# A feed-forward on one core with seven block products in place of eight

## Chip, core and metric

One Trainium2 chip, one core. The metric is the time of one execution on the device, in microseconds. Times come from three runs of the kernel and from one execution with the hardware profiler on.

## What is computed

One layer of a diffusion backbone over 1024 latent tokens (width 1024) with 256 context tokens. A token-mixing sub-layer (a gated linear recurrence and a windowed attention, merged by gates, projected by `w_out`) is added to the stream; then the feed-forward, which is what the change touches:

```python
x_new = x + g1 * _merge(y_hg, y_at, gates, w_branch_hgrn, w_branch_attn, w_out)
h = _modulate(x_new, norm_ffn_w, sh2, sc2)          # (1024, 1024)
out = x_new + g2 * ((silu(h @ w_gate) * (h @ w_up)) @ w_down)
# w_gate, w_up: (1024, 2816); w_down: (2816, 1024); all fp32
```

## The kernel before

Every large product is made from split operands: a value is rounded to `fp32r` (its high part, `act.copy`), the rest is the low part (`dve.tensor_tensor` subtraction), and high x high, high x low and low x high are accumulated in one PSUM bank, three matmuls for one. The matmuls are put in the written order by `InOrder` (L76, L79); on the other engines, and on the queues that issue transfers, a scheduler fixes the order of instructions ahead of the run, from what it takes to be ready first.

Up to about 840 us the kernel does the modulation, the input projections, the attention and the recurrence. Then `gen_ba` (L1048) multiplies the attention branch, L1143 to L1165 multiply the recurrence branch (`bh`) and merge both with gates that are loaded in pairs of pages (`ga`, `gb`), and `project(nh, bs)` (L1238) applies `w_out` to one block of 128 tokens, for one half of 512 columns: 24 matmuls of 512 columns. `project(0, ...)` runs for all blocks, then `project(1, ...)`; after a block's second half, `second_norm` (L1195) squares it (ScalarE), finds the scale (POOL) and scales it (VectorE). `norm_late` (L1256) runs a product and puts the block's eight transposes and its modulation and split (`second_norm_t`, L1209) behind 18 of the 24 matmuls, so block b is transposed inside the product of block b+1; block 6 and block 7 are transposed inside the first two products of the feed-forward.

The feed-forward goes through `w_gate`, `w_up` and `w_down` in 22 blocks of 128 hidden columns. `up(f)` (L1278) loads and splits 512 KB of `w_gate` and of `w_up`, and for each half t of the tokens runs 24 matmuls for the gate and 24 for up (`gemm_ch`, k outer, three terms inner), takes Silu of the gate, multiplies, and splits the result into `ah`, `al`. It also loads a row block of `w_down`, multiplies it by g2 on POOL and splits it. `down(parts, blocks, last)` (L1303) multiplies two such hidden blocks: for each token block and column half 2 x 3 matmuls into one bank; then it adds the bank to the residual page `xn[b]` (L1315), which stays in SBUF. Downs run one pair behind; the last one stores the output (L1317). Weight pages have three buffers (`whi`, `wlo`) and two for what is loaded (`wraw`).

## Time and profile before

| | |
|---|---|
| median of 3 runs | 1756.8 us (1756.18 to 1760.09) |
| the profiled execution | 1757.2 us |
| its span, first to last instruction | 1755.4 us |
| mean granted TensorE clock | 0.985 of full speed |
| instructions | 22971, of which 8820 matmuls |
| DMA | 192.6 MB, mean 110 GB/s |

The rows further down come from the profiled execution. Times are us from the start of the span unless marked ns. PE is TensorE, PEld its weight loads, DVE VectorE, ACT ScalarE, POOL GpSimd, SPq the issuing of transfers on SyncE. L1315 is line 1315 of the kernel before; `out<-in` are the program's tile names, xN a count. Where matmuls are pipelined, the mean of one is its latency, not its spacing.

### The profile page before, as it was taken

The page shows a single profiled execution, that of the slowest core. Times are in us where ns is not written, and L with a number is a line of the kernel's source. Part 1 is how long each engine was busy: PE and PEld are TensorE (multiplying, and loading weights), DVE is VectorE, ACT ScalarE, POOL GpSimd, SP SyncE. Part 2 cuts the span into 40 slices and gives each one's busy share as a digit, 9 for nine tenths or more (in the row PEclk, how much of TensorE's full clock was granted, in tenths as well). Part 3 has the DMA queues.
Part 4 walks back from the last instruction along what each step waited for, and adds up shares of the span by engine and source line. Part 5 has one row for each costly group of instructions (what it writes and reads, how often), then busy time and mean ns, then how long its engine had stood idle before and what let it go on. Part 6 is the DMA issues. An engine that isn't in the chain of part 4 may idle for free. (4 is left out here: it accounts for less than half of the span.)

```text
span 1755.4 us, 22971 instructions
## 1 busy us (share of the span) xinstructions
PE 1692.5 (96%) x8820; PEld 1411.9 (80%) x8820; DVE 958.4 (55%) x1831; ACT 622.7 (35%) x1178; POOL 329.7 (19%) x361
## 2 busy tenths in 40 slices
PE   6899999999889999999899999999999999999999
PEld 4689889998778787788677788888888888888887
DVE  3863577777769697964277462333333433423324
ACT  4312355556546465644543352111112112112110
POOL 2402635310012222321334111010010010010000
PEclk8899999999999999999999999999999999999999
DMA  9771312123277465623555102111112112112102
GB/s 366 252 278 39 110 45 86 46 85 118 93 239 239 133 232 172 228 96 103 191 182 184 36 26 73 47 49 57 40 48 60 36 49 60 37 48 60 37 12 96
DMA packets 177205, 192.60 MB, mean 110 GB/s; under 512 B 9311, under 2 KB 131264, under 8 KB 177096
## 3 DMA queue, kind: packets, MB, share of 16 engines
q1 hardware_dynamic: 161544, 168.59, 29.8%
q10 hardware_dynamic: 15552, 22.55, 3.5%
q8 instruction: 69, 1.13, 0.3%
q14 instruction: 40, 0.33, 0.1%
HBM read 146.53 MB, written 44.57 MB: 109 GB/s over the span
## 5 line engine op out<-in xcount | busy, mean ns | idle before, releaser
L76 PE MATMUL pu<-h,whi_fu 128*128 128x512 f32 x704 | 216.8, 389 | 0.0
L76 PE MATMUL pg<-h,whi_fg 128*128 128x512 f32 x704 | 216.8, 389 | 0.0
L1296 POOL TENSOR_TENSOR fd<-fd,g 128x1024 f32<-128x1024 f32 x22 | 52.7, 2394 | 589.6 <-DMA fd<-in_w_ffn_down_dram 589.6
L1315 DVE TENSOR_TENSOR xn<-xn,dn 128x512 f32<-128x512 f32 x176 | 119.5, 685 | 76.0 <-PE dn L76 75.8
L76 PEld LDWEIGHTS pg<-h,whi_fg 128*128 128x128 f32 x704 | 132.1, 188 | 27.5
L76 PEld LDWEIGHTS pu<-h,whi_fu 128*128 128x128 f32 x704 | 132.1, 188 | 27.2
L76 PE MATMUL pg<-h,wlo_fg 128*128 128x512 f32 x352 | 136.9, 389 | 0.0
L76 PE MATMUL pu<-h,wlo_fu 128*128 128x512 f32 x352 | 136.9, 389 | 0.0
L76 PE MATMUL dn<-dh,ah 128*128 128x512 f32 x352 | 136.9, 389 | 0.0
L76 PE MATMUL dn<-dl,ah 128*128 128x512 f32 x352 | 136.9, 389 | 0.0
L76 PE MATMUL dn<-dh,al 128*128 128x512 f32 x352 | 136.9, 389 | 0.0
L1289 DVE TENSOR_TENSOR sv<-sv,pu 128x512 f32<-128x512 f32 x44 | 30.3, 688 | 192.7 <-PE pu L76 191.2
L76 PE MATMUL g<-hhi,whi_g 128*128 128x512 f32 x256 | 110.0, 430 | 2.8 <-ACT gs_g L347 2.7
L76 PE MATMUL g<-hhi,wlo_g 128*128 128x512 f32 x256 | 101.4, 396 | 0.0
L76 PE MATMUL g<-hlo,whi_g 128*128 128x512 f32 x256 | 100.9, 394 | 0.0
L1288 ACT ACTIVATE sv<-pg 128x512 f32<-128x512 f32 x44 | 26.0, 592 | 208.5 <-PE pg L76 208.5
L76 PE MATMUL wo<-wop,mh 128*128 128x512 f32 x256 | 79.5, 392 | 0.0
L76 PEld LDWEIGHTS pu<-h,wlo_fu 128*128 128x128 f32 x352 | 66.0, 188 | 13.8
L76 PEld LDWEIGHTS dn<-dh,ah 128*128 128x128 f32 x352 | 66.1, 188 | 13.7
L76 PEld LDWEIGHTS dn<-dh,al 128*128 128x128 f32 x352 | 66.1, 188 | 13.7
L76 PEld LDWEIGHTS dn<-dl,ah 128*128 128x128 f32 x352 | 66.1, 188 | 13.7
L76 PEld LDWEIGHTS pg<-h,wlo_fg 128*128 128x128 f32 x352 | 66.1, 188 | 13.6
(424 smaller groups left out, 3980.6 us busy)
## 6 DMA issues: line engine op xcount, KB each, us to landing
aw<-in_w_ada_dram SPq DMA_DIRECT2D x24, 1024.0 KB, 10.1
wraw_fg<-in_w_ffn_gate_dram SPq DMA_DIRECT2D x22, 512.0 KB, 3.7
wraw_fu<-in_w_ffn_up_dram SPq DMA_DIRECT2D x22, 512.0 KB, 3.6
fd<-in_w_ffn_down_dram SPq DMA_DIRECT2D x22, 512.0 KB, 3.4
wraw_g<-in_w_in_dram SPq DMA_DIRECT2D x16, 512.0 KB, 4.0
gates_d<-gs_g ACTq DMA_DIRECT2D x32, 256.0 KB, 2.3
z<-ff_d SPq DMA_DIRECT2D x8, 640.0 KB, 5.4
x_b<-in_x_dram SPq DMA_DIRECT2D x8, 512.0 KB
```

The lines of the kernel that those rows point to most:

```text
L76: self.chain(nc.tensor.matmul(*a, **k))
L1288: act.activation(sv, pg, AF.Silu)
L1289: dve.tensor_tensor(sv, sv, pu, ALU.mult)
L1296: pool.tensor_tensor(raw, raw, g2, ALU.mult)
L1315: dve.tensor_tensor(xn[b][:, a], xn[b][:, a], ps, ALU.add)
```

## The change

The feed-forward's products are made by a scheme of Strassen and Winograd: both operands are cut into 2 x 2 blocks, and seven products of sums of blocks take the place of eight products of blocks.

Up: `h` is cut into token halves and halves of its 1024 channels, a weight into two 128-column blocks and the same channel halves. `up_pair(p)` treats 256 hidden columns (11 pairs). Seven operands are made of `h` once (HB11 to HB22, each split into a high and a low part of 4 x 512 columns): HB11 and HB21 need the first token half only, the others are made in `second_norm_t` for the blocks of the second half, T1 and T4 from sums kept aside (`keep`) and split in `late_operands`. Per pair and weight, `up_operands` loads the raw 1024 x 256 weight block (1 MB, one buffer per weight), makes four sums and splits seven pages of 4 x 128 columns, one step ahead; `up_step` runs 12 matmuls. A chain keeps three accumulators: z (one product, added to a copy of x), x (products 0, 2, 4, 6) and y (3, 5); copies taken of x and y between products are combined on VectorE. The gate chain and the up chain take turns step by step. `hidden(p)` makes three sums more and a difference, and stores seven hidden operands (256 KB each) to DRAM (`a_d`); `down_sums(p)` loads the two row blocks of `w_down` and stores four sums (`t_d`).

Down: seven products, one after the other (77 units of a product s and a pair p). `prepare(u)` loads a hidden operand and a weight operand (256 KB each) and splits both into one page, six units ahead; eight pages, three double buffers for what is loaded. Each product accumulates over the 11 pairs in four banks, one per token block; `snaps` keeps copies of three products. The multiplication by g2 is done on the result, on VectorE, and the residual blocks, stored to DRAM after the second norm (`xn_d`), are loaded again, added to and stored as the output. The last product runs its last four units bank by bank.

SBUF is laid out anew: one pool `pn` of eleven double pages (n0 to n10), `pmA` and `pmB` of four each, `pt` for small ones. So gates have three double pages and not four, the projection's weights take over pages of `t2` and `yh`, the operands HB and HT those of the projection, and the hidden tiles those of the mixed operands. `norm_late` now also covers block 7's product of the last projection, so block 6 is transposed there. `first_operands()` loads and splits the first two weight blocks during the projection. The vectors m2 move into `vt`.

```diff
+    def region(pools_, tag, shape, dt, name):
+        return pools_[0].tile([P] + shape, dt, tag=tag, bufs=1, name=name)
...
+        gt = region(pn, f"n{8 + ct % 3}", [2, 1024], F32, f"gt{ct}")
+        ga, gb = gt[:, 0], gt[:, 1]
...
+        sp.dma_start(xn_d[b], xn[b])
...
+    HB11, HB21, HT2, HT3, HT1, HT4, HB22 = range(7)
...
+    def split(hi, lo, src):
+        act.copy(hi, src)
+        dve.tensor_tensor(lo, src, hi.bitcast(F32), ALU.subtract)
...
+        if b == 0:
+            hop_tile(HB11, pmB, ("b0", "b1"))
+            hop_tile(HB21, pmB, ("b2", "b3"))
+        if b == 4:
+            hop_tile(HT2, pn, ("n8", "n9"))
+            hop_tile(HT3, pmA, ("a0", "a1"))
+            hop_tile(HB22, pmA, ("a2", "a3"))
+        dst = [quarter(pt.tile([P, 512], F32, tag="tmp", bufs=4, name=f"r{b}_{u}")) for u in range(2)]
...
+            if t == 0:
+                split_h((HB11, HB21)[u], dst[u], c)
+        if t == 0:
+            return
+        def f(o, p):
+            return hop[o][p][:, :, c].bitcast(F32)
+        r12, r22 = dst
+        t1, t4 = keep(1, b), keep(4, b)
+        dve.tensor_tensor(t1, r12, f(HB11, 0), ALU.subtract)
+        dve.tensor_tensor(t1, t1, f(HB11, 1), ALU.subtract)
+        dve.tensor_tensor(t4, r22, t1, ALU.subtract)
+        split_h(HT2, t4, c)
+        dve.tensor_tensor(r12, r22, r12, ALU.subtract)
+        split_h(HT3, r12, c)
+        dve.tensor_tensor(t4, f(HB21, 0), t4, ALU.subtract)
+        dve.tensor_tensor(t4, t4, f(HB21, 1), ALU.add)
+        split_h(HB22, r22, c)
...
+    def late_operands(o, nm):
+        hop_tile(o, pn, ("n4", "n5") if nm == 1 else ("n6", "n7"))
+        for i in range(4):
+            split_h(o, kept[nm, i], slice(i * P, i * P + P))
...
+    def op_page(src, name):
+        pg = wpool.tile([P, 2, 4, P], F32R, tag=("whi", "wlo")[n_ops[0] % 2], name=f"op{name}_{n_ops[0]}")
+        n_ops[0] += 1
+        split(pg[:, 0], pg[:, 1], src)
+        return pg
...
+    def up_operands(w, p, m):
+        if p == 0:
+            yield early[m, 0]
+            yield early[m, 1]
+        raw = region(pn, f"n{m}", [8, 256], F32, f"wr{m}_{p}")
+        sp.dma_start(raw, w[:, p * 256 : p * 256 + 256].rearrange("(k p) m -> p k m", p=P))
+        if m == 0:
+            sums[p] = region(pn, "n10", [2, 2, 4, P], F32, f"ws{p}")
+        s1, s2 = sums[p][:, m, 0], sums[p][:, m, 1]
+        def a(i, j):
+            return raw[:, 4 * j : 4 * j + 4, i * P : i * P + P]
+        nm = f"{m}_{p}"
+        if p:
+            yield op_page(a(0, 0), nm)
+            yield op_page(a(0, 1), nm)
+        dve.tensor_tensor(s1, a(1, 0), a(1, 1), ALU.add)
+        dve.tensor_tensor(s2, s1, a(0, 0), ALU.subtract)
+        yield op_page(s2, nm)
+        dve.tensor_tensor(a(1, 0), a(0, 0), a(1, 0), ALU.subtract)
+        yield op_page(a(1, 0), nm)
+        yield op_page(s1, nm)
+        yield op_page(a(1, 1), nm)
+        dve.tensor_tensor(s2, a(0, 1), s2, ALU.subtract)
+        yield op_page(s2, nm)
+    def up_step(ps, pg, o, first):
+        hi, lo = hop[o]
+        for k in range(4):
+            wh, wl = pg[:, 0, k], pg[:, 1, k]
+            for i, (l, r) in enumerate(((wh, hi[:, k]), (wh, lo[:, k]), (wl, hi[:, k]))):
+                pe.matmul(ps, l, r, start=(first and k == 0 and i == 0), stop=(k == 3 and i == 2),
+                          skip_group_check=True)
+    def up_chain(w, p, m, use, c):
+        ops = up_operands(w, p, m)
+        nm = f"{m}_{p}"
+        nxt = next(ops)
+        yield
+        x = mm_tile(f"ux_{nm}") if p % 2 == 0 else psF.tile([P, 512], F32, tag="tp", bufs=2, name=f"ux_{nm}")
+        pg, nxt = nxt, next(ops)
+        up_step(x, pg, HB11, True)
+        act.copy(c[:, 0], x)
+        yield
+        pg, nxt = nxt, next(ops)
+        z = psF.tile([P, 512], F32, tag="gu", name=f"uz_{nm}")
+        up_step(z, pg, HB21, True)
+        dve.tensor_tensor(c[:, 0], z, c[:, 0], ALU.add)
+        use(0, c[:, 0])
+        yield
+        pg, nxt = nxt, next(ops)
+        up_step(x, pg, HT2, False)
+        act.copy(c[:, 1], x)
+        yield
+        pg, nxt = nxt, next(ops)
+        y = psF.tile([P, 512], F32, tag="gu", name=f"uy_{nm}")
+        up_step(y, pg, HT3, True)
+        act.copy(c[:, 2], y)
+        yield
+        pg, nxt = nxt, next(ops)
+        up_step(x, pg, HT1, False)
+        dve.tensor_tensor(c[:, 2], x, c[:, 2], ALU.add)
+        use(2, c[:, 2])
+        yield
+        pg, nxt = nxt, next(ops)
+        up_step(y, pg, HT4, False)
+        dve.tensor_tensor(c[:, 1], y, c[:, 1], ALU.add)
+        use(1, c[:, 1])
+        yield
+        up_step(x, nxt, HB22, False)
+        use(3, x)
+        yield
+    def hidden(p, c):
+        a11, a12, a22, a21 = (c[:, i] for i in range(4))
+        q = [wpool.tile([P, 2, 512], F32, tag="wraw", bufs=2, name=f"hs{p}_{i}") for i in range(2)]
+        s1, s2, s4 = q[0][:, 0], q[0][:, 1], q[1][:, 0]
+        dve.tensor_tensor(s1, a21, a22, ALU.add)
+        dve.tensor_tensor(s2, s1, a11, ALU.subtract)
+        dve.tensor_tensor(a21, a11, a21, ALU.subtract)
+        dve.tensor_tensor(s4, a12, s2, ALU.subtract)
+        for o, s in enumerate((a11, a12, s2, a21, s1, a22, s4)):
+            sp.dma_start(a_d[o][p], s)
...
+    def down_sums(p):
+        rows = []
+        for i in range(2):
+            r = pt.tile([P, 1024], F32, tag="ao", bufs=2, name=f"wd{p}_{i}")
+            sp.dma_start(r, w_fd[(2 * p + i) * P : (2 * p + i + 1) * P, :])
+            rows.append(r)
+        b11, b12, b21, b22 = rows[0][:, :512], rows[0][:, 512:], rows[1][:, :512], rows[1][:, 512:]
+        tt = {o: pt.tile([P, 512], F32, tag="tmp", bufs=4, name=f"td{p}_{o}") for o in TD}
+        dve.tensor_tensor(tt[HT1], b12, b11, ALU.subtract)
+        dve.tensor_tensor(tt[HT2], b22, tt[HT1], ALU.subtract)
+        dve.tensor_tensor(tt[HT3], b22, b12, ALU.subtract)
+        dve.tensor_tensor(tt[HT4], b21, tt[HT2], ALU.subtract)
+        for o, i in TD.items():
+            sp.dma_start(t_d[i][p], tt[o])
+    def up_pair(p):
+        cg = region(pn, "n2", [4, 512], F32, f"cg{p}")
+        cu = region(pn, "n3", [4, 512], F32, f"cu{p}")
+        def gate(i, src):
+            act.activation(cg[:, i], src, AF.Silu)
+        def mult(i, src):
+            dve.tensor_tensor(cu[:, i], src, cg[:, i], ALU.mult)
+        chains = [up_chain(w_fg, p, 0, gate, cg), up_chain(w_fu, p, 1, mult, cu)]
+        for s in range(8):
+            for ch in chains:
+                next(ch)
+            if p == 0 and s == 1:
+                while late:
+                    second_norm_t(*late.pop(0))
+            if p == 0 and s == 2:
+                late_operands(HT1, 1)
+                late_operands(HT4, 4)
+            if s == 4:
+                down_sums(p)
+        hidden(p, cu)
...
+    first_operands()
...
-        (norm_late if b < NB - 1 else whole)(project(1, (b,)))
+        norm_late(project(1, (b,)))
         late.append((b, second_norm(b)))
-
...
+    for p in range(NP):
+        up_pair(p)
...
+    pages = [(pmB, f"b{i}") for i in range(4)] + [(pn, "n8"), (pn, "n9"), (pmA, "a0"), (pmA, "a1")]
+    raws = ((pn, "n0"), (pn, "n1"), (pn, "n10"))
+    units = [(s, p) for s in range(NO) for p in range(NP)]
...
+    def prepare(u):
+        s, p = units[u]
+        if u % 2 == 0:
+            pl_, tag = raws[(u // 2) % 3]
+            raw2[0] = region(pl_, tag, [2, 2, 512], F32, f"dr{u}")
+        raw = raw2[0][:, u % 2]
+        sp.dma_start(raw[:, 0], a_d[s][p])
+        if s in TD:
+            wsrc = t_d[TD[s]][p]
+        else:
+            i, h = {HB11: (0, 0), HB21: (1, 0), HB22: (1, 1)}[s]
+            wsrc = w_fd[(2 * p + i) * P : (2 * p + i + 1) * P, h * 512 : h * 512 + 512]
+        sp.dma_start(raw[:, 1], wsrc)
+        pl_, tag = pages[u % len(pages)]
+        pg = region(pl_, tag, [2, 2, 512], F32R, f"dp{u}")
+        split(pg[:, 0], pg[:, 1], raw)
+        ready[u] = pg
...
-    def up(f):
...
-    def down(parts, blocks, last):
...
+    def finish_block(b, h, src, res):
+        a = slice(h * 512, h * 512 + 512)
+        dve.tensor_tensor(src, src, g2[:, a], ALU.mult)
+        dve.tensor_tensor(res, res, src, ALU.add)
+        sp.dma_start(out2[b * P : b * P + P, a], res)
+    def product(ps, pg, j, first, last):
+        c = slice(j * P, j * P + P)
+        for e, (x_, w_) in enumerate(((0, 0), (0, 1), (1, 0))):
+            pe.matmul(ps, pg[:, x_, 0, c], pg[:, w_, 1], start=(first and e == 0), stop=(last and e == 2),
+                      skip_group_check=True)
+    AHEAD, TAIL = 6, 4
+    for u in range(AHEAD):
+        prepare(u)
+    xs = None
+    ys = None
+    for s in range(NO):
+        if s == 0:
+            banks = xs = [mm_tile(f"dx{j}") for j in range(2)] + [
+                psF.tile([P, 512], F32, tag="tp", bufs=2, name=f"dx{j}") for j in range(2, 4)]
+        elif s in (1, 3):
+            banks = ys = [psF.tile([P, 512], F32, tag="gu", name=f"dy{s}_{j}") for j in range(4)]
+        else:
+            banks = ys if s == 5 else xs
+        done = {1: (0, 0, 0), 4: (1, 1, 3), 5: (1, 0, 2), 6: (0, 1, None)}.get(s)
+        res = []
+        fresh = s in (0, 1, 3)
+        n_tail = TAIL if s == NO - 1 else 0
+        for p in range(NP - n_tail):
+            u = s * NP + p
+            if u + AHEAD < len(units):
+                prepare(u + AHEAD)
+            if p == 2 and done:
+                rt = region(pn, "n7", [4, 512], F32, f"res{s}")
+                for j in range(4):
+                    t, h = done[:2]
+                    b = 4 * t + j
+                    sp.dma_start(rt[:, j], xn_d[b][:, h * 512 : h * 512 + 512])
+                    res.append(rt[:, j])
+            pg = ready.pop(u)
+            for j in range(4):
+                product(banks[j], pg, j, fresh and p == 0, p == NP - 1)
+        tail = [ready.pop(s * NP + p) for p in range(NP - n_tail, NP)]
+        if s in snap_at:
+            pl_, tag = snap_at[s]
+            snaps[s] = region(pl_, tag, [4, 512], F32, f"snap{s}")
+        for j in range(4):
+            for i, pg in enumerate(tail):
+                product(banks[j], pg, j, False, i == len(tail) - 1)
+            if s in snap_at:
+                act.copy(snaps[s][:, j], banks[j])
+                continue
+            t, h, other = done
+            b, a = 4 * t + j, slice(h * 512, h * 512 + 512)
+            if other is None:
+                cb = pt.tile([P, 512], F32, tag="tmp", bufs=4, name=f"c{b}")
+                dve.tensor_tensor(cb, banks[j], g2[:, a], ALU.mult)
+                dve.tensor_tensor(res[j], res[j], cb, ALU.add)
+                sp.dma_start(out2[b * P : b * P + P, a], res[j])
+            else:
+                cb = pt.tile([P, 512], F32, tag="tmp", bufs=4, name=f"c{b}_{h}")
+                dve.tensor_tensor(cb, banks[j], snaps[{0: 0, 3: 3, 2: 2}[other]][:, j], ALU.add)
+                finish_block(b, h, cb, res[j])
```

## Rows read from the trace of the kernel before

**Rows 1.** Page: busy us, share of span, instructions by engine.
```profile
PE 1692.5 (96%) x8820; PEld 1411.9 (80%) x8820; DVE 958.4 (55%) x1831; ACT 622.7 (35%) x1178; POOL 329.7 (19%) x361
```

**Rows 2.** Chain of waits by time: start us, us, engine, tile, line.
```profile
1031.77 4.08 PE pg L76 x18
...
1098.84 10.88 PE dn L76 x48
1109.71 5.44 PE pg L76 x24
...
1718.99 32.65 PE dn L76 x144
...
1751.67 0.69 DVE xn L1315
```

**Rows 3.** Stretches: us; busy PE, PEld, DVE, ACT, POOL; granted clock, DMA share, GB/s.
```profile
20.00:30.00 10.00, 8.79 (x48) 4.91 (x49) 4.03 (x9) 4.01 (x6) 1.38 (x1) 0.66 1.05 408
...
840.00:860.00 20.00, 14.40 (x57) 11.42 (x56) 2.75 (x3) 9.81 (x13) 6.66 (x5) 0.83 0.84 301
...
848.00:852.00 4.00, 0.00 (x0) 0.00 (x0) 0.00 (x0) 2.61 (x3) 0.00 (x0) 0.64 1.01 369
...
1300.00:1400.00 100.00, 100.00 (x443) 82.81 (x442) 34.58 (x46) 15.12 (x20) 7.19 (x3) 1.00 0.14 42
```

**Rows 4.** Groups by form, 1044 to 1756: busy us, mean ns, idle before.
```profile
L76 PE MATMUL dn<-dh,ah 128*128 128x512 f32 x352 | 136.9, 389 | 0.0
...
L1315 DVE TENSOR_TENSOR xn<-xn,dn 128x512 f32<-128x512 f32 x176 | 119.5, 685 | 76.0 <-PE dn L76 75.8
...
L1293 DVE TENSOR_TENSOR al<-sv,ah 128x512 fp32r<-128x512 f32 x44 | 30.3, 689 | 14.9 <-ACT ah L1292 14.9
...
L1292 ACT CAST ah<-sv 128x512 fp32r<-128x512 f32 x44 | 27.3, 619 | 97.9 <-DVE sv L1289 97.9
...
L136 DVE TENSOR_TENSOR wlo_fg<-wraw_fg,whi_fg 128x1024 fp32r<-128x1024 f32 x20 | 24.5, 1225 | 11.6 <-ACT whi_fg L135 10.0
...
L135 ACT CAST whi_fg<-wraw_fg 128x1024 fp32r<-128x1024 f32 x20 | 21.1, 1053 | 86.7 <-DMA wraw_fg<-in_w_ffn_gate_dram 43.8 <-issue 39.0 <-PE pu L76 3.9
```

**Rows 5.** Tile wraw_fg: issues on SP, ns min, median, max.
```profile
L143 SPq DMA_DIRECT2D wraw_fg<-in_w_ffn_gate_dram x22: 367/368/379, 956.0 to 1650.5; - x22
```

**Rows 6.** DMA issues: count, KB each, us to landing.
```profile
aw<-in_w_ada_dram SPq DMA_DIRECT2D x24, 1024.0 KB, 10.1
wraw_fg<-in_w_ffn_gate_dram SPq DMA_DIRECT2D x22, 512.0 KB, 3.7
...
out_dram<-xn SPq DMA_DIRECT2D x16, 256.0 KB, 2.0
...
zq<-qh_d SPq DMA_DIRECT2D x8, 256.0 KB, 4.6
```

**Rows 7.** Timeline of one block in the projection: start us, us.
```profile
1011.25 2.90 ACT L1218 ACTIVATE tm<-tp,m 128x128 f32<-128x128 f32 x8 [2.50 <-issue]
...
1013.03 0.69 DVE L1252 TENSOR_TENSOR xn<-xn,wo 128x512 f32<-128x512 f32 x1
...
1014.00 0.67 ACT L1199 ACTIVATE xh<-xn 128x512 f32<-128x512 f32 x1
...
1016.58 0.88 DVE L1206 TENSOR_SCALAR xh<-xn,rs 128x512 f32<-128x512 f32 x2 [1.44 <-POOL rs L1204]
...
1017.12 1.09 PE L79 MATMUL tp<-ident,xh 128*128 128x128 f32 x8
```

**Rows 8.** Waits of PE, 840 to 1030: us, times, longest.
```profile
PE ba L76 <- ACT t L1069: 6.3, 2, 5.6
PE tp L79 <- DVE xh L1206: 2.3, 2, 2.1
```

More of the change, by code (lines that the diff above doesn't have):

```diff
@@ L1186, in tile_hybrid_block @@
     for b in range(NB):
-        xb = page(pr, F32, "xn", f"xn{b}", 8)
-        sp.dma_start(xb, x2[b * P : (b + 1) * P, :])
-        xn.append(xb)
+        if b % 2 == 0 and b < 6:
+            xb = region(pn, f"n{8 + b // 2}", [2, 1024], F32, f"xn{b}")
+        xt = pt.tile([P, 1024], F32, tag="ao", bufs=2, name=f"xn{b}") if b >= 6 else xb[:, b % 2]
+        sp.dma_start(xt, x2[b * P : (b + 1) * P, :])
+        xn.append(xt)
     wos.append(w_out_half(1))
-    h2 = {}
     ss2 = const.tile([P, 2 * NB], F32, name="ss2")
     rs2 = const.tile([P, NB], F32, name="rs2")
+    xn_d = [dram.tile([P, D], F32, name=f"xn_d{b}") for b in range(NB)]
     def second_norm(b):
@@ L1260, in norm_late, with first_operands @@
                 second_norm_t(*late.pop(0))
+    NP = NFF // 2
+    NO = 7
+    a_d = [dram.tile([NP, P, 512], F32, name=f"a_d{o}") for o in range(NO)]
+    t_d = [dram.tile([NP, P, 512], F32, name=f"t_d{o}") for o in range(4)]
+    n_ops = [0]
+    def op_page(src, name):
[3 more added lines that the diff above has]
+        return pg
+    early = {}
+    def first_operands():
+        for m, w in enumerate((w_fg, w_fu)):
+            raw = wpool.tile([P, KT, P], F32, tag="wraw", bufs=2, name=f"we{m}")
+            sp.dma_start(raw, w[:, 0:P].rearrange("(k p) m -> p k m", p=P))
+            early[m] = raw
+        for i in range(2):
+            for m in range(2):
+                early[m, i] = op_page(early[m][:, 4 * i : 4 * i + 4], f"e{m}")
@@ L1303, in down @@
-    def down(parts, blocks, last):
-        for b in blocks:
-            t, o = b // 4, (b % 4) * P
-            for nh in range(2):
-                a = slice(nh * 512, nh * 512 + 512)
-                ps = psF.tile([P, 512], F32, tag="tp", bufs=2, name=f"dn_{b}_{nh}") if nh else mm_tile(f"dn_{b}_{nh}")
-                i = 0
-                for ah, al, dh, dl in parts:
-                    xh, xl = ah[t][:, o : o + P], al[t][:, o : o + P]
-                    for l, r in ((xh, dh[:, a]), (xh, dl[:, a]), (xl, dh[:, a])):
-                        pe.matmul(ps, l, r, start=(i == 0), stop=(i == 3 * len(parts) - 1))
-                        i += 1
-                dve.tensor_tensor(xn[b][:, a], xn[b][:, a], ps, ALU.add)
-                if last:
-                    sp.dma_start(out2[b * P : b * P + P, a], xn[b][:, a])
@@ L1319, in tile_hybrid_block @@
-    prev = None
-    for sg_ in range(NFF // 2):
-        cur = []
-        for i in range(2):
-            cur.append(up(2 * sg_ + i))
-            if prev is not None:
-                down(prev, range(4 * i, 4 * i + 4), False)
-        prev = cur
-    down(prev, range(NB), True)
+    for p in range(NP):
[3 more added lines that the diff above has]
+    units = [(s, p) for s in range(NO) for p in range(NP)]
```

160 lines of the change are left out of this document (76 added, 84 removed).

## The prediction, made before the changed kernel was run

> **What bounds the kernel now.** I read the shares of the engines first: TensorE is busy 96% of the span, VectorE 55%, ScalarE 35% [rows 1]. That alone proves little, since matmul ends are modelled, so I went to the chain of waits in order of time. From 1031.8 us on it holds nothing but matmuls, in pieces that never vary: 24 matmuls of a gate or up product in 5.44 us, 48 of the down product in 10.88 us, 144 of the last down in 32.65 us, then one VectorE addition and the stores [rows 2]. So one 512-column matmul costs 10.88 / 48 = 0.2267 us with no gap, the feed-forward takes 1751.7 - 1031.8 = 719.9 us, and 3168 matmuls times 0.2267 is 718.1 us of that. The stretch 1300 to 1400 says the same: PE 100 of 100 us at granted clock 1.00, VectorE 34.6, ScalarE 15.1, DMA share 0.14 [rows 3]. What counts is therefore the number of matmuls, and whether the other engines can still feed them.
>
> **What goes.** Gate and up: 22 column blocks x 2 halves x 2 weights x 24 = 2112 matmuls; down: 8 x 2 x 11 pairs x 6 = 1056. After: 11 pairs x 2 weights x 7 products x 12 = 1848, and 7 products x 11 units x 12 = 924, in all 2772 of the same shape (128x128 against 128x512) and the same three-term order. 396 fewer x 0.2267 = **-89.8 us**, if the new ones run at the old spacing. The Trainium skill ("TensorE: Matmul & The Clock Gate", Back-to-back issue gap) gives some 216 ns for an isolated 512-column matmul and 131 ns in a sustained stream; by these 396 would be worth 85.5 or 51.9 us (estimates from that page). The chain shows 226.7 ns with no gap, above both, and the measurement decides.
>
> **What comes in the up phase.** Per pair of column blocks PE needs 14 x 12 x 0.2267 = 38.1 us. VectorE gets, per pair: 8 weight sums, 14 weight splits, 6 combinations of products, 4 gate multiplications, 4 sums of the hidden operands, 4 sums of down weights: 40 instructions of 512 elements at 0.69 us [rows 4], 27.6 us, 72%. ScalarE gets 14 split copies, 6 copies out of PSUM and 4 Silu: 24 x 0.62 = 14.9 us. POOL loses the 22 multiplications by g2. The queue of SP issues 15 transfers of up to 0.37 us each [rows 5], 5.6 us, in which 6.0 MB move: 158 GB/s, where the trace moved 408 GB/s at full load [rows 3]. None of these exceeds PE, so the totals cost nothing; the cover is PE's 38.1 us, and if it were gone VectorE's 27.6 us would be the bound.
>
> What could still cost is order. A weight page has three slots per chain, so the page of step s+2 can be filled once step s-1 is done: two steps of both chains plus one, 13.6 us, for one copy (0.62) and one subtraction (0.69). A PSUM bank that keeps accumulating (x after 0, 2, 4; y after 3) has the other chain's step and one more step between its evacuation and its next matmul, over 5.4 us against 0.69. The raw weights of a chain have a single buffer: the 1 MB load of the next pair waits for the last split out of it. The page of that split takes the slot of the third product, which is free after step 3 of 7; the load then has about four steps (20 us) for an issue, a landing between 3.7 us (512 KB) and 10.1 us (1 MB, nearly all of them in the crowded first stage) [rows 6], and 1.3 us of split. I take zero, from the first rows' side, and keep the other end as a rival. On SP the loads could stand behind the seven stores of the hidden operands, which wait for VectorE; queued behind those are only the next raw weights and the down weights. At the end of a pair, the up chain's first copy into its tile waits for those stores, about 6 us after the last matmul, while PE needs that bank again only 13 us after it: hidden.
>
> **The start of the feed-forward.** Here VectorE and ScalarE are not idle. In the projection before it a block's chain runs from its addition (1013.03) through two squares, POOL and the scaling to the transposes at 1017.12, 4.1 us [rows 7], against the 18 matmuls (4.08 us) that stand before the transposes: no slack at all, PE waited 2.3 us there in sum [rows 8]. For the first four blocks the change moves the high parts from VectorE to ScalarE (two copies of 0.62), in front of the next block's squares: 1.0 to 1.4 us later per block, so 4 to 5.6 us. For the last four it adds six additions or subtractions and replaces sixteen small ones: 9 x 0.69 + 0.69 + 0.88 = 7.8 us of VectorE per block against PE's 6.5 us; at best they slip past each other (0), at worst the scaling waits for all of them (3.4 us, for three blocks). Block 6's transposes also move before the feed-forward, into the last projection, where the cover is 4.1 us and not a gate product. Bounds 0 and 16 us; I take **+6**, nearest to the ScalarE part, which no gap can take up.
>
> In the first pair, HB11 and HB21 (10.9 us, both chains) cover block 7. Then VectorE must finish its nine sums, the late operands (eight subtractions, 5.5 us), and the weight sums and splits of two steps, some 18 us of work where PE offers about 13 before the second step after. Bounds 0 (all in gaps) and 10; I take **+5**. These waits are of a few us, and where PE waited 5.6 us (at 848, [rows 8]) the granted clock fell to 0.64 in that stretch and stood below 1.00 in its surroundings [rows 3]; I add nothing for it.
>
> **Up to down.** The first units read a11 and rows of w_fd, both there before the up phase ends; pages b0 to b3 are free after the second step of the last pair. The bank of the last up product is free one 0.69 us multiplication after its matmul, with 0.68 us of the first bank's work in front: **+0.3**.
>
> **Down.** Per unit PE 12 x 0.2267 = 2.72 us, VectorE 1.23, ScalarE 1.05 [rows 4], SP two issues of up to 0.37. Two 256 KB loads per unit are 193 GB/s, half of the 408 GB/s shown [rows 3], and six units (16 us) lie between a load and its use, against a landing of 2.0 (stores at the end) to 4.6 us (in the busy middle) [rows 6]: nothing. Snapshots and additions into the result fall beside 30 us steps. At the very end a bank takes two operations and not one: **+0.7**.
>
> **Before the feed-forward** the memory is laid out anew: gates have three double pages and not four, and lie where the recurrence's buffers were. PE waits 5.6 us at 848 for a ScalarE copy that stands behind gate work while DMA is full [rows 3, 8]; that can go or grow. Taken 0, bounds -8 and +8.
>
> **Sum.** 1757.2 (the profiled execution, span 1755.4, against a median of 1756.8 of the runs) - 89.8 + 6 + 5 + 0.3 + 0.7 = **1679.4**.
>
> **Rivals.** (a) Short waits in every pair: the order on VectorE and SP is fixed ahead, and 72% busy leaves bursts (five VectorE operations at the end of a pair, four in the middle). One 2 to 6 us wait per pair, 11 times, gives 22 to 66 us: 1701 to 1745. Against it: windows of 13 us for 1.3 us of work.
> (b) The raw weights come too late: with loads of the next pair issued behind the stores of the hidden operands, PE waits per pair for one multiplication (0.69), four sums (2.8), seven issues (2.6), a landing of 3.7 to 10.1 and a split (1.3), together 11.1 to 17.5 us, ten times: 111 to 175 us, 1790 to 1854, **slower**. It decides from 78 / 10 = 7.8 us per pair. For it: one buffer per chain, and a queue whose order is fixed ahead. Against: the loads are free to be issued some 20 us earlier.
> (c) The 256 KB loads of the down do not overlap: 2 x 2.0 us per unit instead of 2.72 gives 77 x 1.28 = 99 us, 1778, slower; at 4.6 us each far slower. It decides from 3.7 us per unit. Against: the trace moved 369 GB/s with several 512 KB gate loads in flight at 848 [rows 3]. The Trainium skill ("DMA: Bandwidth & Descriptors", Measured) advises at least 1 MiB per transfer for 75% of peak, and its fit of 2.0 us plus bytes over 436 GB/s gives 2.6 us for 256 KB; taken one after the other this would be 5.2 us per unit and 1870 us, an estimate from that page. The trace bears out the fixed part (2.0 us for 256 KB), not the serial use.
> (d) The start costs nothing and the wait at 848 goes: 1757.2 - 89.8 + 1 - 8 = 1660.
>
> **How the numbers follow.** The forecast case (1662 to 1697) 0.62; (a) 0.20, of which three quarters lie below 1718; (b) 0.07; (c) 0.04; (d) and below 0.04; something that just gives the gain back 0.03. The range 1662 to 1718 holds 0.62 + 0.15 and a part of (d), close to 8 in 10. No change here means within 0.2% (3.5 us), about what a measurement of this kernel can tell. Faster 0.86, same 0.02, slower 0.12.
>
> **What would show it.** Right: feed-forward matmuls in the chain in pieces of 12 x 0.2267 = 2.72 us, pairs of 38.1 us, 209 us of down, some 10 us of PE waits between 985 and 1075. (a) shows as PE waits on VectorE or ScalarE pages in every pair; (b) as ScalarE waiting for the DMA of the raw weights at each pair's start, with SP idle in front of a store; (c) as a DMA share near 1 in the down with PE waiting. The forecast is wrong if the pairs are longer than 40 us, or if the start costs over 20.

## The result and the profile after

The changed kernel takes **1695.0 us** (median of 4 runs, 1694.26 to 1698.77) against 1756.5 us for the kernel before on the same chip (1755.97 to 1760.09): ratio 0.965, 95% interval 0.9631 to 0.9669, a gain of 61.5 us. Forecast were 1679.4 us and a gain of 77.8 us from the profiled execution; the range, 1662 to 1718, holds the result. A second series gave 1691.7 us, ratio 0.9634 (0.9616 to 0.9653). The profiled execution is the slowest of the first series: 1698.77 us, span 1697.0.

The page's shares of the engines, to be read beside [rows 1]:

```profile
PE 1609.2 (95%) x8424; PEld 1341.9 (79%) x8424; DVE 1111.1 (65%) x2018; ACT 758.7 (45%) x1405; POOL 284.6 (17%) x339
```

396 matmuls fewer; VectorE has 153 us more, ScalarE 136. TensorE still decides, as the chain of waits shows, which answers to [rows 2] (start us, us, engine, tile, line, count):

```profile
1172.02 10.88 PE ux L76 x48
1182.90 5.44 PE uz L76 x24
...
1483.35 29.56 PE dx L76 x129
1512.91 29.92 PE dy L76 x132
...
1662.51 29.93 PE dx L76 x132
1692.47 0.70 DVE c L1592
1693.19 0.69 DVE res L1593
```

From 1151 us on it holds matmuls, 24 in 5.44 us and 132 in 29.92, that is 0.2267 us each, as before. There are two exceptions: the last two operations of VectorE, and the 26 us before the down stage (up to 1483.35). In these the chain runs through loads and splits of the first down operands, as in the row below, while TensorE has other products to do and waits only 0.6 us:

```profile
1460.83 5.40 DMA dr<-in_w_ffn_down_dram
```

Most of what was lost lies before 1151 us. The stretches (us; busy PE, PEld, DVE, ACT, POOL; granted clock, DMA share, GB/s) show it beside the steady state, to be read beside [rows 3]:

```profile
1036.00:1042.00 6.00, 3.77 (x14) 3.32 (x15) 5.53 (x10) 4.32 (x12) 1.39 (x2) 0.72 1.00 332
1042.00:1048.00 6.00, 5.71 (x25) 4.35 (x24) 6.00 (x11) 5.37 (x12) 1.03 (x1) 0.99 0.78 279
1048.00:1054.00 6.00, 1.74 (x9) 1.77 (x10) 5.00 (x10) 0.93 (x3) 3.42 (x3) 0.86 0.08 12
1054.00:1060.00 6.00, 6.00 (x24) 4.89 (x24) 5.95 (x11) 5.94 (x14) 0.00 (x0) 0.86 0.45 169
1060.00:1066.00 6.00, 1.20 (x3) 0.29 (x1) 6.00 (x11) 3.75 (x5) 0.00 (x0) 0.71 0.36 131
1066.00:1072.00 6.00, 4.27 (x10) 3.40 (x11) 5.25 (x9) 0.62 (x1) 0.00 (x0) 0.50 0.64 212
...
1300.00:1400.00 100.00, 100.00 (x443) 82.81 (x442) 59.90 (x94) 37.55 (x64) 0.00 (x0) 1.00 0.30 106
1500.00:1600.00 100.00, 100.00 (x442) 82.79 (x442) 52.17 (x49) 42.35 (x46) 0.00 (x0) 1.00 0.65 214
```

The first pair of the up phase starts at 1042.1 us. There VectorE is busy 5 to 6 of every 6 us, TensorE stands, and its granted clock falls to 0.50, the lower of its two levels (1.2 GHz). The same place in TensorE's timeline, with the wait and what ended it in brackets:

```profile
1042.11 5.60 PE L76 MATMUL ux<-hop,ope 128*128 128x512 f32 x24
1052.26 1.91 PE L79 MATMUL tp<-ident,xh 128*128 128x128 f32 x8 [4.55 <-DVE xh L1223]
1053.81 6.60 PE L76 MATMUL uz<-hop,ope 128*128 128x512 f32 x24
1064.78 0.79 PE L76 MATMUL ux<-hop,op 128*128 128x512 f32 x1 [4.37 <-ACT hop L1240]
1067.73 7.85 PE L76 MATMUL ux<-hop,op 128*128 128x512 f32 x23 [2.17 <-DVE hop L1241]
1075.42 5.60 PE L76 MATMUL uy<-hop,op 128*128 128x512 f32 x24
```

23 matmuls take 7.85 us after the third wait, where 24 take 5.60 later. All waits of TensorE from 930 to 1700 us, to be read beside [rows 8] (us, times, longest):

```profile
PE tp L79 <- DVE xh L1223: 12.0, 7, 4.5
PE ux L76 <- ACT hop L1240: 4.4, 1, 4.4
PE bh L76 <- DVE gt L1173: 4.3, 2, 2.7
PE ux L76 <- DVE hop L1241: 2.2, 1, 2.2
PE ux L76 <- ACT cu L1407: 2.1, 1, 2.1
PE dx L76 <- DVE cu L1476: 0.6, 1, 0.6
```

Last, why block 7's scaling (xh) comes so late. POOL's and VectorE's timelines around 1047 us:

```profile
1046.97 3.71 POOL L1219 TENSOR_TENSOR rs<-ss 128x1 f32<-128x1 f32 x1 [9.41 <-ACT xh L1216]
```
```profile
1046.93 1.28 DVE L1241 TENSOR_TENSOR hop<-kt,hop 128x512 fp32r<-128x512 f32 x2
...
1049.94 0.68 DVE L1241 TENSOR_TENSOR hop<-kt,hop 128x512 fp32r<-128x512 f32 x1
1051.62 0.88 DVE L1223 TENSOR_SCALAR xh<-xn,rs 128x512 f32<-128x512 f32 x2 [1.00 <-POOL rs L1221]
...
1054.83 0.68 DVE L1461 TENSOR_TENSOR td<-wd 128x512 f32<-128x512 f32 x1
...
1063.39 0.68 DVE L1296 TENSOR_TENSOR kt<-r,kt 128x512 f32<-128x512 f32 x1
```

An addition of one column on POOL, which took 0.19 to 0.20 us for blocks 2 to 4 and 0.48 and 0.65 for blocks 5 and 6, took 3.71 and ended at 1050.68, where VectorE's unbroken run ended (1049.94 + 0.68 = 1050.62). And L1461, a sum for the *down* stage, due 430 us later, stands ahead of L1296, which T2 of block 7 and with it TensorE waits for.

### The profile page after: what moved, and what is told of

Its sections match the earlier page's. It is cut to its first block, busy times and chain, and to the rows that moved or that the text cites. A ratio compares the mean times of both kernels' runs of the same rounds, so it can differ in the third digit from the quotient of the medians.

```text
span 1697.0 us, 23284 instructions
## 1 busy us (share of the span) xinstructions
PE 1609.2 (95%) x8424; PEld 1341.9 (79%) x8424; DVE 1111.1 (65%) x2018; ACT 758.7 (45%) x1405; POOL 284.6 (17%) x339
## 4 chain that ended last, share of the span: by engine, by line
PE 36%; DMA 5%; DVE 4%; ACT 2%; issue 2%; POOL 1%; SPq 0%; POOLq 0%; ACTq 0%; DVEq 0%
PE ux L76 10%; PE dx L76 7%; PE dy L76 5%; PE uy L76 5%; PE wo L76 3%; PE uz L76 3%; DMA wd<-in_w_ffn_down_dram 2%; PE ba L76 1%; ACT r L1282 1%; PE bh L76 1%; DMA gt<-gates_d 1%; DMA dr<-in_w_ffn_down_dram 1%; DMA wr<-in_w_ffn_up_dram 1%; ACT xh L1216 0%; DVE mx L1176 0%
## 5 line engine op out<-in xcount | busy, mean ns | idle before, releaser
L76 PE MATMUL ux<-hop,op 128*128 128x512 f32 x1032 | 244.2, 394 | 8.6 <-ACT hop L1240 4.4
L76 PEld LDWEIGHTS ux<-hop,op 128*128 128x128 f32 x1032 | 196.5, 191 | 51.1 <-ACT hop L1240 4.8
L1241 DVE TENSOR_TENSOR dp<-dr,dp 128x1024 fp32r<-128x1024 f32 x77 | 93.9, 1223 | 85.1 <-ACT dp L1240 77.6
L1240 ACT CAST dp<-dr 128x1024 fp32r<-128x1024 f32 x77 | 81.0, 1052 | 117.6 <-PE dy L76 49.1
L76 PE MATMUL uy<-hop,op 128*128 128x512 f32 x528 | 123.3, 389 | 0.0
L76 PE MATMUL dx<-dp 128*128 128x512 f32 x528 | 120.6, 389 | 0.6 <-DVE cu L1476 0.6
L76 PEld LDWEIGHTS dx<-dp 128*128 128x128 f32 x528 | 99.0, 188 | 21.6 <-DVE cu L1476 1.0
L76 PEld LDWEIGHTS uy<-hop,op 128*128 128x128 f32 x528 | 99.1, 188 | 20.6
L76 PE MATMUL wo<-wop,mx 128*128 128x512 f32 x384 | 90.4, 395 | 0.0
L76 PE MATMUL dy<-dp 128*128 128x512 f32 x396 | 90.2, 389 | 0.0
```

The source lines that it names most:

```text
L76: self.chain(nc.tensor.matmul(*a, **k))
L1240: act.copy(hi, src)
L1241: dve.tensor_tensor(lo, src, hi.bitcast(F32), ALU.subtract)
```

## The experiments

Every kernel is the changed one with an edit; c0 is the changed kernel's second series, the control of e5, e6 and e7. A ratio is to the kernel before on the same chip. The stages come from each kernel's profiled execution: project from its first matmul to the first of the up phase; pair 0 and pairs 1 to 10 of the up phase; down to its last matmul. Bare matmuls would be 38.1 (and 1.1 of transposes), 380.8 and 209.5 us. There is one profile of each kernel, and kernels whose program is the same in a stage show how far a stage can be trusted: project 102.0 to 103.9 us (changed, c0, e1, e4, e5, e6, e8), pair 0 54.9 to 56.5 (changed, c0, e5, e6).

| kernel | time us | ratio to before, 95% | project | pair 0 | pairs 1-10 | down |
|---|---|---|---|---|---|---|
| before | 1756.5 | 1 | 96.0 | | | |
| changed, first | 1695.0 | 0.965 (0.9631-0.9669) | 103.6 | 55.1 | 384.7 | 210.5 |
| c0 changed | 1691.7 | 0.9634 (0.9616-0.9653) | 103.4 | 54.9 | 382.0 | 210.1 |
| e1 sums held | 1689.3 | 0.961 (0.9593-0.9628) | 103.9 | 52.0 | 380.8 | 210.1 |
| e2 scale on VectorE | 1694.4 | 0.9634 (0.9621-0.9647) | 102.5 | 58.0 | 382.2 | 210.1 |
| e3 copies on VectorE | 1686.7 | 0.959 (0.9574-0.9606) | 100.1 | 54.6 | 380.8 | 210.1 |
| e4 fill | 1692.1 | 0.9626 (0.9607-0.9644) | 103.4 | 55.1 | 381.8 | 210.1 |
| e5 no turns | 1697.6 | 0.9664 (0.9644-0.9685) | 102.0 | 56.5 | 388.7 | 210.0 |
| e6 one raw buffer | 1789.5 | 1.0188 (1.0168-1.0209) | 103.9 | 55.4 | 384.7 | 303.5 |
| e7 = e1 + e3 | 1685.2 | 0.9594 (0.9576-0.9612) | 99.6 | 51.6 | 380.8 | 210.1 |
| e8 = e1 + e5 | 1694.3 | 0.964 (0.9626-0.9654) | 103.1 | 52.7 | 385.7 | 210.0 |
| e9 = e7 + T4 on POOL | 1684.4 | 0.9579 (0.9566-0.9593) | 96.7 | 56.0 | 380.8 | 210.1 |
| e10 = e7 + fill | 1682.1 | 0.957 (0.9555-0.9586) | 99.9 | 50.4 | 380.8 | 210.1 |
| e11 = e7 + fill + order | 1677.9 | 0.9547 (0.9529-0.9565) | 97.4 | 50.0 | 380.8 | 210.1 |

**c0, the changed kernel again.**

> The changed kernel itself, beside the others of this batch: it should come out within 4 us of its 1695.0, and say by how much the kernels of the two batches can be set against it. If its project stage starts at 933 to 934 us of the span, as in the four kernels of the first batch, the 3 to 5 us before the project stage that the first profile of the changed kernel showed belong to that one execution and not to the change.

1691.7 us, 3.3 us below the first series. Its project stage starts at 936.6 us; over all these profiles it starts between 933.0 and 938.6 with the same code up to there. So the 3 us by which it starts later in the first profile (938.6 against 935.6 before) lie within this spread and can't be put down to the change, though the expected 933 to 934 was too narrow.

**e1, the sums of the down weights held back.**

```diff
+            st = sp.dma_start(a_d[o][p], s)
+        return st
...
-            if s == 4:
-                down_sums(p)
-        hidden(p, cu)
+        down_sums(p, hidden(p, cu))
...
+            after(sp.dma_start(r, w_fd[...]), behind)
```

> Theory S (VectorE is full in the first pair, and sums of down weights that nothing needs for hundreds of us stand in its queue there): with each pair's down sums held behind that pair's hidden stores, some four sums (2.4 us) leave the stretch before the second wait, so the two waits for the T2 operand (4.4 and 2.2 us) shrink to about 3 in all; the 2.1 us wait for the copy into the up tile in the second pair goes too, as the stores no longer share DMA with loads run ahead; with the clock that is lost less, 4 to 9 us under the changed kernel (1686 to 1691). Rival L (the raw weight pages that come free only with the last projection set the start): nothing before the second pair moves, at most 2 us off in all.

As theory S had it: the two waits for T2 fell from 6.6 to 3.2 us, pair 0 took 52.0 us, and the wait on `cu` is gone from pairs 1 to 10. By the whole time alone e1 and c0 can't be told apart (their intervals overlap); the stages tell them apart. The stretch 1100 to 1140 us of the changed kernel (first fence) and of e1 (second; columns as above) shows what left:

```profile
1100.00:1140.00 40.00, 40.00 (x178) 33.14 (x177) 31.62 (x52) 14.12 (x26) 0.00 (x0) 1.00 0.85 295
```
```profile
1100.00:1140.00 40.00, 40.00 (x178) 33.14 (x178) 27.23 (x45) 14.73 (x25) 0.00 (x0) 1.00 0.45 161
```

The scheduler, which issues what is ready, had brought the sums of later pairs and their loads forward into the one place where VectorE was full: in the changed kernel all 44 sums of the eleven pairs (L1461 to L1464) are done by 1169 us, in e1 only eight are by 1150 us and the last four come after 1480. The wait on `cu` needs more than that, though. It stands in the changed kernel, c0, e2 and e4, not in e3 and e6, whose sums run ahead too.

**e2, block 7's scale on VectorE and ScalarE.**

```diff
+        eng = dve if b == 7 else pool
...
+            dve.reciprocal(r, r)
+            act.activation(r, r, AF.Sqrt)
```

> Block 7's scale is found on VectorE and ScalarE (a square root there) and not on POOL. If POOL is held up by VectorE's dense run (one addition of a single column took 3.7 us there, 0.2 elsewhere), the wait of 4.5 us before block 7's transposes falls to about 2, less 1.3 us for a table of the square root; what follows is still VectorE's, so 0 to 3 us in all. If POOL was late for another reason (its input came late), the wait stays at 4 to 5 us and the time the same.

A miss: the wait for the transposes rose to 9.85 us. The three one-column operations now stood in VectorE's own queue (1045.44, 1047.92 and 1049.19 us), each between operations of 0.69 us; an activation-table load of 1.28 us on ScalarE ran beside them, from 1048.13 us. The sum of squares had been there since 1042.40, so the first of the three stood 3 us in the queue. The wait for T2 shrank in turn, and the time did not move. So what POOL's 3.71 us cost by themselves e2 does not show: it moved the same work into the queue that was full.

**e3, the high parts of blocks 0 to 3 back on VectorE.**

```diff
-                split_h((HB11, HB21)[u], dst[u], c)
+                hi, lo = [t_[:, :, c] for t_ in hop[(HB11, HB21)[u]]]
+                dve.tensor_copy(hi, dst[u])
+                dve.tensor_tensor(lo, dst[u], hi.bitcast(F32), ALU.subtract)
```

> High parts of the first four blocks made by VectorE again. If the two ScalarE copies in front of the squares are the cost of the projection's steps (theory of the prediction), the four waits of 1.1 us before transposes of blocks 1 to 4 fall to 0.1 to 0.3, 3 to 4 us faster than the changed kernel. If VectorE is what these chains wait for, it gets eight instructions more: no gain, or 1 to 2 us slower.

As expected: project 100.1 us, 3.5 less, and of seven waits for transposes three are left:

```profile
PE ux L76 <- ACT hop L1240: 7.0, 1, 7.0
PE tp L79 <- DVE xh L1223: 5.7, 3, 2.8
```

Pair 0 hardly gained: what no longer waits at the transposes waits at T2.

**e4, unread matmuls before the two waits of pair 0.**

```diff
+            if p == 0 and s in (1, 2):
+                fill = psF.tile([P, 512], F32, tag="gu", name=f"fill{s}")
+                for i in range(18):
+                    pe.matmul(fill, hop[HB11][0][:, 0, 0:P], hop[HB11][0][:, 0], start=True, stop=True)
```

> 18 matmuls that nothing reads are put in front of each of the two long waits of the first pair (4.1 us each, against waits of 4.5 and 6.5). If the clock that falls in these waits costs what the first pair lost beyond its waits (55.1 - 38.1 - 1.1 - 11.1 = 4.8 us), the granted clock stays at 1.00 and 3 to 5 us are gained. If it costs nothing, the time stays or grows by up to 2 us, as the fill stands in front of work that is ready.

The waits fell from 11.1 to 5.1 us and the clock stayed at 0.97 or more from 1042 to 1061 us, then fell to 0.50 as before; pair 0 took 55.1 us, to the tenth what it took without. TensorE was kept fast, but had no operand: T2 could go on 26.3 us after the start of the pair, without the fill after 25.6.

**e5, pairs 1 to 10 without turns.**

```diff
+        if p:
+            for ch in chains:
+                for s in range(8):
+                    next(ch)
+            down_sums(p)
+            hidden(p, cu)
+            return
```

> Pairs 1 to 10 run gate's seven products and then up's; only the order of the steps is put back. Theory T (taking turns pays): within one chain a bank that is accumulated, copied and accumulated again is needed again after one step of 2.72 us and its evacuation of 0.6 to 0.7 us plus the queue stands in between, and up's multiply waits for gate: TensorE gets waits of 0.2 to 1 us a step, 10 to 60 us in all over 140 steps, time 1705 to 1755. Theory N (the seven products alone pay): the copy falls under the product that writes another bank, so no wait of TensorE longer than now, time within 4 us of the changed kernel.

Pairs 1 to 10 took 388.7 us, 6.7 more than the control, in few and early waits on the additions into the banks (1091 to 1481 us):

```profile
PE ux L76 <- DVE cu L1426: 3.2, 2, 2.9
PE ux L76 <- DVE cg L1426: 1.4, 2, 1.2
PE uy L76 <- ACT cu L1422: 0.2, 1, 0.2
```

From 1174 us on every pair but the last (39.1) took 38.08 us here too. So neither theory held: there is no wait in every step, and the time, 5.9 us over the control, is not within 4 us of it either.

**e8, the same with the sums held** (e1's and e5's edits). It asks whether turns pay only where the sums run ahead.

> Pairs 1 to 10 without turns, as before, and the sums of the down weights held behind hidden. Without turns alone the up stage took 445.2 us against 436.9 of the control; all of the difference lay in pairs 0 to 2, where waits on VectorE's additions into the banks (2.93 and 1.19 us) and the clock after them cost some 7 us, and from 1172 us on a pair took 38.08 us as with turns. Theory Q (turns pay only where VectorE's queue is full of sums run ahead): with the sums held the up stage is 432.8 us give or take 1.5, as with turns, time 1687 to 1692 us. Theory T (turns pay by themselves): the waits on the additions stay, up stage 438 us or more, time 1694 us or more.

Theory T held: the up stage took 438.4 us, and pairs 1 to 10 took 385.7, 4.9 more than with turns. The waits are now spread, one of up to 1.5 us at the same place of pairs 1 to 9 (the last pair waits elsewhere), where the bank of HT1 must be free for HB22 one step (2.72 us) later:

```profile
1299.73 5.78 PE L76 MATMUL ux<-hop,op 128*128 128x512 f32 x24 [0.54 <-DVE cg L1426]
...
1415.69 5.74 PE L76 MATMUL ux<-hop,op 128*128 128x512 f32 x24 [1.21 <-DVE cg L1426]
```

So the waits go where the sums go: in e5 the sums had all run ahead and only pairs 1, 2 and the last paid; here each pair carries its own. With turns there are three steps (8.16 us) between, and e1 shows no such wait. The turns are worth some 5 to 7 us.

**e6, one raw buffer in the down stage.**

```diff
-    raws = ((pn, "n0"), (pn, "n1"), (pn, "n10"))
+    raws = ((pn, "n0"),)
```

> The down stage loads its pairs of operand units through one raw buffer in place of three. Theory O (the depth of three hides the loads): with one, load (about 2 us for 256 KB at the rates seen, and the queue), split (two copies and two subtractions) and product follow one another, and a pair of units takes 6 to 8 us in place of 5.44, +40 to +190 us on the 210 us of the stage, all of it TensorE waiting for a load or a split. Theory P (the load was never near): the load and the splits of the next pair fit under one pair of products even with a single buffer, since the splits release the raw buffer early: within 4 us, and the prediction's case of loads one behind the other was never close.

As theory O had it: the down stage took 303.5 us, 7.88 per two units (77 / 2 of them) for 5.46. The chain of waits of e6 shows a cycle without a matmul in it:

```profile
1607.79 1.06 ACT dp L1240
1608.87 1.24 DVE dp L1241
1610.12 0.32 SPq L1517
...
1610.48 0.43 SPq L1523
...
1610.96 0.43 SPq L1517
...
1611.43 4.25 DMA dr<-t_d
```

Split, free the buffer, issue four loads, wait for the last. The loads overlap one another: four of some 4 us each fit into a cycle of 7.9. But no load of the next two units starts before the second split of these two has freed the buffer. The depth in buffers is thus worth 93 us; the Trainium skill ("DMA: Bandwidth & Descriptors", Measured) asks for larger transfers, and no run here changed their size.

**e7, e1 and e3 together.**

> Both edits that gained, together: the sums of the down weights behind hidden (first batch: 52.0 us for pair 0, 432.8 us for the up stage) and the high parts of the first four blocks copied by VectorE (project stage 3.6 us shorter). If the two touch different waits, they add: about 5.7 + 8.3 less the 2 to 4 us of the second that came from pair 0's and the cu wait, so 1681 to 1685 us. If both relieve the same queue of VectorE at the start of the up stage, the sum is no better than the copies alone: 1686 to 1688 us.

1685.2 us: between the two theories, and no clear gain over e3 alone (the intervals overlap). By stages the edits do add (project 99.6, pair 0 51.6), but this profile's project stage starts at 937.7 us, e3's at 933.7.

**e9, T4's last two operations of blocks 4 to 7 on POOL.**

```diff
-        dve.tensor_tensor(t4, f(HB21, 0), t4, ALU.subtract)
-        dve.tensor_tensor(t4, t4, f(HB21, 1), ALU.add)
+        pool.tensor_tensor(t4, f(HB21, 0), t4, ALU.subtract)
+        pool.tensor_tensor(t4, t4, f(HB21, 1), ALU.add)
```

> The version with both edits, and for blocks 4 to 7 the two last operations on the activations' T4 on POOL in place of VectorE: 8 of 0.68 us each less for VectorE, 8 of 1.6 us more for POOL. Theory V (what is left in pair 0 is VectorE's queue and nothing else): the two for block 6 and the two for block 7 are out of the way of T2's last operand, which comes 1.4 to 2.7 us earlier; up stage 430 to 431 us, time 1682 to 1684 us. Rival W (the two engines get in each other's way, as POOL's one-column additions showed): the POOL operations take over 3 us each beside a dense VectorE, or stand ahead of block 7's scale on POOL, the transposes wait longer, and the up stage takes 433 to 440 us.

Both happened, in different places: the project stage fell to 96.7 us, near the 96.0 before the change, and pair 0 rose to 56.0. The up stage's 436.8 us is what the rival named; the time is that of e7. POOL's timeline, then VectorE's:

```profile
1049.48 4.06 POOL L1302 TENSOR_TENSOR kt<-hop,kt 128x512 f32<-128x512 f32 x1 [10.09 <-DVE hop L1241]
```
```profile
1052.33 0.68 DVE L1414 TENSOR_TENSOR cu<-uz,cu 128x512 f32<-128x512 f32 x1
1052.93 1.16 DVE L1241 TENSOR_TENSOR op<-wr,op 128x512 fp32r<-128x512 f32 x1
1054.01 1.75 DVE L1241 TENSOR_TENSOR op<-ws,op 128x512 fp32r<-128x512 f32 x1
```

An operation that took 1.29 us for blocks 4 and 5 and 1.66 for block 7 took 4.06. If it ran in its last 1.29 us, it began at 1052.25, beside VectorE's L1414, one of whose inputs (`uz`) lies in PSUM; the next two of VectorE's, both inputs in SBUF, are then stretched from 0.68 to 1.16 and 1.75 us. For block 5 (1034.23 us) it is the same: VectorE's L1325, with `wo` in PSUM, took 0.67 us beside POOL's operation, the next one, with both inputs in SBUF, 1.40.

**e10, e7 with 10 and 32 unread matmuls.**

> The version with both edits, with unread matmuls issued before the two long waits of pair 0 (10 and 32). Theory C (part of what is left is the clock that falls in these waits): the granted clock stays at 0.9 to 1.00 from 1042 to 1072 us, where it was 0.50 and 0.65, the first 23 matmuls after the wait take 5.2 us in place of 7.6, and the up stage goes from 432.4 to 429.5 to 430.5 us, time 1681 to 1683 us. Rival V (only VectorE's queue counts): the clock is kept and the up stage stays at 432 to 433 us, because the operands of the next products come no earlier than before.

The clock was 1.00 in every stretch from 1036 us on, the 23 matmuls after the wait took 5.51 us, and pair 0 50.4, 1.2 less than in e7; the up stage, 431.1 us, lies between the two theories. In e7 pair 0 loses 3.0 us beyond matmuls, transposes and waits (51.6 - 38.1 - 1.1 - 9.4). Of these only 1.2 came back, since T2 could go on only 23.2 us after the start of the pair, in e7 after 22.4. The 1.2 us are no more than the spread of pair 0 between kernels with the same program there.

**e11, VectorE's queue put in order.** From e10, fill 10 and 20: a list holds block 7's last subtraction for T2, and what VectorE gets after it in the program is tied behind it.

```diff
+    def held(ins):
+        if t2_done:
+            after(ins, t2_done[0])
+        return ins
...
+        last = split_h(HT2, t4, c)
+        if b == 7:
+            t2_done.append(last)
+        held(dve.tensor_tensor(r12, r22, r12, ALU.subtract))
...
```

> The version with both edits and unread matmuls (10 and 20), and VectorE's queue put in order before T2: once block 7's low part of T2 is set, and not before, come the rest of block 7's T operands, the late operands' splits and the weights' parts for the steps after T2. In the version before, block 7's four operations for T2 stood from 1047.10 to 1057.33 us with 13 others of 0.68 us between them. Theory V (what is left of pair 0 is the order of VectorE's queue): some 6 to 9 of those 13 move behind, T2's operand comes 4 to 6 us earlier, and as the moved ones are due only one to three steps of 5.44 us later, the up stage goes from 431.1 to 426 to 428 us, time 1677 to 1680 us. Rival B (the same amount of work is only late elsewhere): the wait moves to the products after T2, whose operands now come late, and the up stage stays at 430 to 433 us.

T2 now runs without a wait from 1053.11 us; in e10 all but its first matmul came from 1058.66 us on, with 12 unread matmuls (2.7 us) more ahead of it. But now T3 waits, as TensorE's timeline shows:

```profile
1053.11 5.60 PE L76 MATMUL ux<-hop,op 128*128 128x512 f32 x24
1058.55 0.39 PE L76 MATMUL uy<-hop,op 128*128 128x512 f32 x1
1061.22 7.13 PE L76 MATMUL uy<-hop,op 128*128 128x512 f32 x23 [2.29 <-DVE hop L1241]
```

and VectorE's says for what: seven splits of the late operands, due one and two steps after T3, came first of what was held, then T3's weights, and only at 1060.48 us the low part of block 7 for T3 itself, whose end at 1061.17 lets TensorE go on.

```profile
1053.26 4.30 DVE L1241 TENSOR_TENSOR hop<-kt,hop 128x512 fp32r<-128x512 f32 x7
1057.47 1.29 DVE L1241 TENSOR_TENSOR op<-wr,op 128x512 fp32r<-128x512 f32 x2
...
1060.48 0.69 DVE L1241 TENSOR_TENSOR hop<-r,hop 128x512 fp32r<-128x512 f32 x1
```

Rival B: up stage 430.8 us. The time, 1677.9 us, is nevertheless the lowest of all, though its interval overlaps e10's, mostly through a project stage of 97.4 us, 2.5 less than in e10. In this stage the wait before block 6's transposes is 1.57 us for 2.80, POOL's one-column addition ahead of it took 0.65 for 1.86, and the granted clock from 1026 us to the end of the stage is 1.00 for 0.82; which of the holds did this was not tested. e11 computes what the changed kernel computes and is 4.5% faster than the kernel before.

## Why the prediction was right, and where it was off

Its sum against the first profile: 1757.2 - 89.8 leaves 1667.4; the profile took 1698.8. The terms measured: 3.0 before the project stage, 7.6 in it, 17.0 in pair 0, 3.9 in pairs 1 to 10, 1.0 in down, 0.7 at the end (4.5 us after the last matmul, 3.8 before), less 1.9 of transposes and gaps that the feed-forward before had too (720.0 - 718.1): 31.3, as it should be. Forecast were 12 for all of this. The median, 1695.0, lies 2 us below the upper end of the forecast case (1697), the profiled execution as much above it.

By its own signs the prediction was in part wrong. "The forecast is wrong if the pairs are longer than 40 us, or if the start costs over 20": the start cost 24.6 (7.6 + 17.0); pair 0 took 55.1 us and pair 2 42.0, the other nine 38.08. The waits of TensorE between 985 and 1075 us are 18.6 us, not some 10. The number holds because the matmuls, the largest term, came out as forecast, and because the forecast case left 18 us above its value.

**The matmuls, -89.8: right.** 12 of them took 2.72 us in up and down. The Trainium skill ("TensorE: Matmul & The Clock Gate", Back-to-back issue gap) would have made it 51.9 or 85.5 (estimates from that page); the row stands at 0.2267 us per matmul in the new order too.

**Project, +6: right, by its cause.** 7.6 measured; four waits of 1.06 to 1.11 us stand where 1.0 to 1.4 per block were forecast, and e3, which takes the copies off ScalarE, removes them and 3.5 us of the stage. The rest is blocks 5 and 6 behind VectorE's sums (waits of 0.85 and 2.25 us); e9, which takes two operations per block off VectorE, makes the stage 2.9 us shorter than e7.

**First pair, +5 with bounds 0 and 10: the step that failed.** 17.0 less 1.1 of transposes is 15.9. Of these, 11.1 are waits and 4.8 what products and transposes took longer at the lower clock. The step counted 18 us of VectorE's work against 13 of TensorE's, and let HB11 and HB21 (10.9 us) cover block 7; but its transposes stand behind HB11 alone (5.4 us) and waited 4.55 us there. Three things more were not in it. Block 6, transposed only at 1038 us, still filled most of VectorE's time up to 1050.62 us. What is ready is put in early, so that sums due hundreds of us later stood in the same queue: holding them gives back 3 us here, in e1 against the changed kernel and in e7 against e3. And POOL's scale for block 7 was held up by VectorE; what this cost by itself no run shows. "I add nothing for it", of the clock, was near in what it is worth: with the clock at 1.00 (e10) pair 0 takes 1.2 us less. What is left, about 11 us over the bare products in e10 and e11, is VectorE's work as it falls due: VectorE is busy nearly all the time from 1036 to 1060 us in both, and putting one product's operands first made the next one's late. That this remainder can't be had by a still better order was not shown.

**Up phase steady, 0: right but for one wait.** Every kernel with turns whose sums are held takes 380.8 us. Of those whose sums run ahead, e3 does too, e6 waits only before its first down product (3.78 us), and the others lose 1.0 to 3.9, all of it in pairs 1 and 2. The reason given, the steps that lie between a bank's evacuation and its next use, is the one that e5 and e8 bear out, at 5 to 7 us; they are three steps, 8.16 us, where the prediction counted two. VectorE was busy 68% of a stretch in e1 (1300 to 1400 us), near the 72% of the sum.

**Down, 0 and +0.3, and +0.7 at the end: right** (1.0, of which the first matmul's wait is 0.6; and 0.7). It rested on the loads being issued six units ahead; e6 shows what three raw buffers are worth for that, 93 us.

**Rivals.** No wait in every pair (a), no wait for raw weights (b), no wait in down (c): DMA share there 0.65, 214 GB/s. Rival (c) had nearly the price of e6 (1778 against 1789.5) by luck: its mechanism is loads that don't overlap, and what makes them late in e6 is the buffer they wait for. In (d), the wait at 848 us stayed (4.97 us at 857.8).

## What to carry to other kernels

Counting an engine's work over a stage was nearly enough for the steady state here; at a border between stages count what is left over of the stage before and what a scheduler may pull forward from the stages after, since both stand in the same queue. Tie work that is due much later behind something late, with a dependency, before trying to speed up what waits. Order what is tied by when it is due, too, or the wait moves one product on, as in e11. And a filler that keeps the clock up buys little while the operands are what is missing.

## What was not expected of the hardware

POOL was held up by a dense VectorE. POOL's one-column addition, 0.19 us where VectorE paused, took 3.71 us for block 7 in seven kernels (changed, c0, e1, e4, e5, e6, e8) and 1.86 for block 6 in four (e1, e2, e3, e10). Each time it ended within 0.1 us of the end of VectorE's unbroken run, in the changed kernel after six of VectorE's operations. It need not wait that long: for blocks 5 and 6 of the changed kernel it took 0.48 and 0.65 and ended behind the one operation that VectorE had running, with no pause of VectorE's over 0.05 us there, and in e7, where the run had a gap of 0.07 us near it, 0.43. What decides between the two no run shows. In e9 a 1.29 us operation of POOL ran beside VectorE's operations with an input in PSUM without stretching them, and stretched the next ones, with both inputs in SBUF, by 0.48 and 1.07 us (block 6) and by 0.7 (block 5). The Trainium skill ("SBUF — State Buffer", SBUF: two separate sides) says that the two engines share a pair of ports as an exclusive lock, taken by a VectorE operation with two SBUF inputs against one of POOL that reads SBUF, and that the loser blocks; these rows agree with it.
